# A block-diagonal step for the state chain, and the loads, norm and tanh of a head pair moved beside the former pair's inverse

## The chip, the cores and the metric

The kernel runs on one core of a Trainium2 chip. The time is device microseconds of one execution of the whole program; the median of several runs counts. The core's engines are TensorE (PE, matmuls, with PEld for its weight loads), VectorE (DVE), ScalarE (ACT), GpSimd (POOL) and SyncE (SP, which here only issues DMAs). Each takes its instructions strictly in the order in which they stand in its own queue and waits on semaphores where it needs another engine's result. Matmul results go to PSUM, which the kernel divides into banks.

## The reference

One layer of a recurrent decoder for 1024 prompt rows and 64 sample rows (8 groups of 8 rows). A dense input projection gives the columns of three branches; one of them is a recurrence over heads of 64, with a 64x64 state per head.

```python
h = rms_norm(x) * (1 + sc) + sh
P = h @ w_in                       # 1024 x 4352, split in recurrent, pooling and gate columns
# recurrent branch, per head, r, w = decay, k, v, kk (normalised), a per row t:
def step(S, inp):
    sa = einsum("bhvk,bhk->bhv", S, -kk_t)
    S = S * w_t + sa * (kk_t * a_t) + v_t * k_t
    return S, einsum("bhvk,bhk->bhv", S, r_t)
decay = exp(-exp(-softplus(-(w0 + tanh(xw) @ w2)) - 0.5));  a = sigmoid(a0 + xa @ a2)
kk = kk * rsqrt(sum(kk * kk) + 1e-12)
# pooling branch: running means over 2/4/8/16 rows; gates: sigmoid
merged = g_r * (o_r @ w_br_rwkv) + g_p * (o_p @ w_br_pool)
x = x + gt * (merged @ w_out);  x = x + gt * (relu(h2 @ w_ff1)**2 @ w_ff2)
```

The prompt's 1024 rows are handled in 16 chunks of 64 rows: within a chunk the recurrence is solved by a triangular inverse, and from chunk to chunk only the state S is carried: S_next = diag(end) S + (a 64x64 matrix) S + (a term without S), where `end` is the chunk's decay. The 8 heads are taken as 4 pairs: a pair fills the 128 partitions, head 0 in the lower 64 and head 1 in the upper 64.

## The kernel before

**Two kinds of work.** The first half of the run (to some 770 us) is the dense projection: `products` issues, job by job, matmuls of 128x128 weights with 362 or 364 rows (operand names `hx` and `whi`, `wlo`; tag `mm`). The weights come by SP's queue as `wraw`; ScalarE splits off `whi` (L193) and VectorE or GpSimd `wlo` (L194). A job's results are copied out of PSUM by ScalarE, with a tanh for the gate columns (L564), as plain copies for the pooling columns (L582). The recurrent branch needs some of the projected columns and runs beside the rest of them: `heads` (below), `chains`, and `pools`, in which VectorE forms the sums of the windows (L601, L602) and small products `px,plw` follow. After these, products on the merged rows (`mr`), the output projection and the MLP follow in the second half.

**What sets the order.** TensorE's order is written by hand through a clock of planned TensorE time, `Pace`: the dense stream (`back`) and the three other tasks (`fore`) are generators; a task that yields a number of nanoseconds is taken up again when that much planned matmul time has gone by, one that yields a function when that is true. `Pace.warm(t)` also waits for enough dense work before. The other engines' orders come from a scheduler, which lays the instructions by its own estimates. So the numbers in the yields set the place of a piece of work between the dense matmuls, and the other queues follow.

**The pairs.** For pair f, `front(f)` loads the projected columns k, kk, wa and r from DRAM, shifts and mixes rows through transposes (`spread`, L177 with `kct`, and `wt,sw` products), forms the norm (`rinv`, L347 to L362: products with two columns, a square root on ScalarE, a reciprocal on VectorE, and copies of the result by ScalarE, L360), takes two tanh out of PSUM (L677, L680), and then works out the decay by a scan (L698) and the decayed keys `bk` (L710, L711). `scores` and `unit` make the score products `ra,bk` for chunks of four, read out by VectorE (L794, L795) and ScalarE (L800, L802). `inverse` and `level` solve the triangles, `affine` makes for each of two units of 8 chunks the matrices of the state step: its `first` makes `w` and `uv`, its `second` two groups of products `ab,at` read out by ScalarE (L960) and VectorE (L961). `sample(f)` does the 64 sample rows (products `x,z` and `ab,uv`, readers L1028 to L1067), `post(f)` the normalisation and output gate of the pair (L1113 to L1118).

`heads` puts them together: `lead` (front and scores of f) runs merged with `sample(f-1)`, then `main` (inverse, level, affine of f) merged with `post(f-1)`. `chains` runs `chain(f)` from the time that the first unit of pair f is ready: 16 steps, one each 2300 ns of planned time (1500 in the last pair), so beside `lead` of the next pair. One step, for both heads of a pair (`pn` collects the next state, `py` the output rows, `ra[:, i, 1]` holds the matrix and `ra[:, i, 0]` the output weights):

```python
for hs in HB:                                   # HB: partitions 0-63, 64-127
    self.mm(pn[hs, at], ra[hs, i, 1, :], S[hs, :], ...)
nc.vector.scalar_tensor_tensor(S1, S, end[:, c:c + 1], pn[:, at], op0=ALU.mult, op1=ALU.add)
for hs in HB:
    self.mm(py[hs, at], S[hs, :], ra[hs, i, 0, :], ...)
```

**PSUM.** Tag `mm` has four banks (dense), `wc` two (pn and py of the chain), `w` two, for everything else of the heads: a group of products with tag `w` must wait until the group before the last one has been read out.

## Time and profile before

| what | value |
| --- | --- |
| median of three runs | 1656.83 us (1656.82 to 1659.11) |
| profiled execution | 1654.8 us, of it the span 1653.0 |
| TensorE busy | 1597.1 us, 97% of the span |
| VectorE, ScalarE, GpSimd busy | 1040.3, 721.7, 364.6 us |
| mean granted TensorE clock | 0.991 |

The profile is of one execution. Busy time is the time in which an engine runs an instruction; a line such as "PE w L170 <- ACT wt L677: 5.7, 8, 2.0" among the waits says that TensorE (its matmuls of tag w, issued at line 170) stood idle for 5.7 us in total, 8 times, at most 2.0 us at once, until ScalarE's instruction of line 677, which writes or reads wt, was done. In a timeline row stand the start, the duration, the engine, line and operation, output and inputs, the sizes, and in brackets the idle time before and what ended it. Line numbers are those of the kernel before, unless said otherwise; from L363 on the changed kernel's are 2 higher, from L680 some 10 to 16, from the chain on 21 to 23.

### The profile page before, as it was taken

How to read it: one execution, taken by the hardware profiler on the slowest of the kernel's cores; microseconds unless marked ns; L12 is line 12 of the kernel's file. 1: busy time of each engine (PE TensorE's matmuls, PEld its weight loads, DVE VectorE, ACT ScalarE, POOL GpSimd, SP SyncE). 2: the span in 40 equal slices, each digit the busy share in tenths (PEclk: the TensorE clock that was granted, in tenths of full speed). 3: DMA queues.
4: the chain of work that ended last, by engine and by line, in shares of the span. 5: the costliest groups of instructions: out<-in, count | busy, mean ns of one | idle time of the engine just before them, and what ended most of it. 6: DMA issues, size and time to landing. Idle time of an engine off the chain costs nothing.

```text
span 1653.0 us, 35432 instructions
## 1 busy us (share of the span) xinstructions
PE 1597.1 (97%) x14331; PEld 1488.8 (90%) x14331; DVE 1040.3 (63%) x1800; ACT 721.7 (44%) x1414; POOL 364.6 (22%) x459
## 2 busy tenths in 40 slices
PE   6999999999999999999999999999999999999997
PEld 3989878887888889979989999999999999999997
DVE  5686547744675466334553696777555677877866
ACT  5543333343334333412233475545444765553323
POOL 3320101100000000001631332323233342521231
PEclk9999999999999999999999999999999999999999
DMA  9333413331332242375976455666665965675313
GB/s 338 111 110 135 139 48 119 117 102 67 113 109 92 80 136 102 103 295 174 348 251 227 131 181 180 220 226 240 232 222 204 347 202 190 195 247 182 99 39 109
DMA packets 123333, 279.43 MB, mean 169 GB/s; under 512 B 16769, under 2 KB 31105, under 8 KB 123169
## 3 DMA queue, kind: packets, MB, share of 16 engines
q1 hardware_dynamic: 107808, 228.52, 40.4%
q0 software_dynamic: 9312, 32.41, 5.9%
q10 hardware_dynamic: 6048, 16.23, 2.8%
q8 instruction: 113, 1.85, 0.5%
q14 instruction: 52, 0.42, 0.1%
HBM read 198.15 MB, written 78.95 MB: 168 GB/s over the span
## 4 chain that ended last, share of the span: by engine, by line
PE 82%; DVE 7%; ACT 4%; DMA 3%; issue 3%; POOL 1%; SPq 0%; DVEq 0%; ACTq 0%; POOLq 0%
PE mm L170 36%; PE pr L170 30%; PE w L170 11%; PE wc L170 4%; DMA wraw<-in_w_out 1%; PE w L177 1%; DVE hx L1729 1%; DMA x<-in_xT 1%; ACT whi L193 1%; DVE wlo L194 1%; DVE bk L711 0%; DVE wt L698 0%; POOL wlo L194 0%; DVE bk L710 0%; DMA wr<-in_w_ff 0%
## 5 line engine op out<-in xcount | busy, mean ns | idle before, releaser
L170 PE MATMUL mm<-hx,whi 128*128 128x362 f32 (+1 forms) x1920 | 507.8, 346 | 6.8 <-ACT px L564 2.9
L170 PEld LDWEIGHTS mm<-hx,whi 128*128 128x128 f32 x1920 | 334.0, 190 | 43.2 <-issue 18.5
L170 PE MATMUL pr<-mr,whi 128*128 128x272 f32 x1792 | 336.5, 287 | 0.6 <-DVE hx L1729 0.6
L170 PE MATMUL mm<-hx,wlo 128*128 128x362 f32 (+1 forms) x960 | 316.1, 329 | 0.0
L170 PEld LDWEIGHTS pr<-mr,whi 128*128 128x128 f32 x1792 | 280.7, 188 | 2.8 <-issue 2.8
L170 PE MATMUL pr<-mr,wlo 128*128 128x272 f32 x896 | 257.9, 288 | 0.2 <-DVE wlo L194 0.2
L193 ACT ACTIVATE whi<-wraw 128x512 fp32r<-128x512 f32 x186 | 116.9, 630 | 232.3 <-PE mm L170 68.9
L194 DVE TENSOR_TENSOR wlo<-wraw,whi 128x512 fp32r<-128x512 f32 x145 | 112.1, 773 | 121.1 <-ACT whi L193 120.9
L170 PEld LDWEIGHTS mm<-hx,wlo 128*128 128x128 f32 x960 | 182.9, 190 | 0.0
L170 PE MATMUL pr<-hx,whi 128*128 128x272 f32 x896 | 168.7, 287 | 1.4 <-DVE rs L1924 0.8
L170 PEld LDWEIGHTS pr<-mr,wlo 128*128 128x128 f32 x896 | 168.6, 188 | 0.4 <-DVE wlo L194 0.4
L170 PE MATMUL mm<-mr,whi 128*128 128x272 f32 (+4 forms) x736 | 152.3, 301 | 0.0
L170 PEld LDWEIGHTS pr<-hx,whi 128*128 128x128 f32 x896 | 140.3, 188 | 2.6 <-ACT whi L193 1.0
L193 ACT ACTIVATE whi<-wr 128x512 fp32r<-128x512 f32 x138 | 86.4, 628 | 112.6 <-PE pr L170 80.4
L170 PE MATMUL pr<-hx,wlo 128*128 128x272 f32 x448 | 128.9, 288 | 0.0
L170 PEld LDWEIGHTS mm<-mr,whi 128*128 128x128 f32 x736 | 119.2, 188 | 3.0 <-issue 2.5
L170 PE MATMUL mm<-mr,wlo 128*128 128x272 f32 (+4 forms) x368 | 110.2, 299 | 0.0
L194 POOL TENSOR_TENSOR wlo<-wraw,whi 128x512 fp32r<-128x512 f32 x41 | 55.3, 1349 | 245.8 <-ACT whi L193 245.6
L194 DVE TENSOR_TENSOR wlo<-wr,whi 128x512 fp32r<-128x512 f32 x103 | 77.2, 752 | 17.4 <-ACT whi L193 17.3
L170 PE MATMUL pr<-t,whi 128*128 128x272 f32 x448 | 84.6, 287 | 0.0
L170 PEld LDWEIGHTS pr<-hx,wlo 128*128 128x128 f32 x448 | 84.3, 188 | 0.0
L170 PEld LDWEIGHTS pr<-t,whi 128*128 128x128 f32 x448 | 70.2, 188 | 0.8 <-issue 0.8
(398 smaller groups left out, 2704.9 us busy)
## 6 DMA issues: line engine op xcount, KB each, us to landing
wr<-in_w_ff SPq DMA_DIRECT2D x137, 256.0 KB, 3.4
hid<-d_ch POOLq DMA_DIRECT2D x72, 272.0 KB, 3.7
wraw<-in_w_ff SPq DMA_DIRECT2D x71, 256.0 KB, 3.1
wraw<-in_w_in SPq DMA_DIRECT2D x68, 256.0 KB, 3.0
d_ch<-hx SPq DMA_DIRECT2D x52, 272.0 KB, 3.7
hid<-in_w_ada_mlp SPq DMA_DIRECT2D x24, 512.0 KB, 6.6
d_th<-px SPq DMA_DIRECT2D x22, 544.0 KB, 2.9
wt<-d_x SPq DMA_DIRECT2D x20, 544.0 KB, 4.3
```

Of the source, the lines that this page charges most:

```text
L170: return self.nc.tensor.matmul(out, lhsT, rhs, **kw)
L177: self.nc.tensor.transpose(out, in_, ident)
L193: nc.scalar.activation(hi, raw, AF.Copy)
L194: (nc.gpsimd if pool else nc.vector).tensor_tensor(lo, raw, hi.bitcast(F32), op=ALU.subtract)
L1729: nc.vector.tensor_tensor(acc, acc, v, op=ALU.add)
```

## The change

Four edits, in the order of the code.

1. `rinv` ends with a tanh of one column, whose result nobody reads; it loads ScalarE's table for the tanh.
2. `front` is split. `front(f)` keeps the loads, mixing, norm and tanh, with 1900 and 2000 ns after a tanh instead of 1300; the scan and the decayed keys become `burst(f)`, in which pieces are 1800, 1700 and 1400 ns apart for f > 0 (they had none between). `heads` runs `front(0)` ahead of all, and `front(f+1)` behind `post(f-1)`, so beside inverse, level and affine of pair f; `lead` holds `burst` and `scores`. The first unit of the scores starts 3000 instead of 9000 ns later for f > 0, and `warm` asks 12000 ns instead of 8000.
3. The chain's step has one product per output in place of two: `pn` from the block-diagonal 128x128 matrix `ra[:, i, 1:3]`, to which the chunk's decay has been added on the diagonal, and `py` from `sbd`, a 128x128 tile with the two heads' states on its diagonal. ScalarE copies the new state from PSUM to S, GpSimd copies its two halves into `sbd`.
4. `affine` builds that matrix: `ra` has a third plane, `at` now lies there, GpSimd makes the diagonal of the decay (`dg`) and clears the off-diagonal blocks, VectorE adds the products to the diagonal in place of ScalarE's copy. In `first` the copy of one half of `uv` goes from VectorE to ScalarE.

```diff
@@ -352,3 +352,4 @@
             self.mm(ps[:, 2 * i:2 * i + 2], x[:, b:b + 128], self.kc("hsel"), start=True, stop=True)
-        r = self.cp.tile([P, 9, 2], F32, tag="rh", bufs=3, name=self.nm("rh"))[:, :k, :]
+        r = self.cp.tile([P, 10, 2], F32, tag="rh", bufs=3, name=self.nm("rh"))
+        last, r = r[:, 9, 0:1], r[:, :k, :]
         f = r.rearrange("p k h -> p (k h)")
@@ -361,2 +362,3 @@
             i += m
+        nc.scalar.activation(last, R[-1][:, 0:1], AF.Tanh)
         return [x[:, o:o + 128] for x in R for o in range(0, x.shape[1], 128)]
@@ -664,3 +666,3 @@
         t1, tha = self.wt(), self.wt()
-        yield self.pace.warm(8000 if f else 11000)
+        yield self.pace.warm(12000 if f else 11000)
 
@@ -680,3 +682,3 @@
             nc.scalar.activation(tha[:, c0:c0 + n], ps[:, :n], AF.Tanh, bias=self.hp[:, 4 + f:5 + f], scale=0.5)
-            yield 1300
+            yield 1900 if c0 else 2000
         yield X(f)
@@ -684,2 +686,10 @@
         nc.sync.dma_start(r, self.d_x[f])
+        self.cur = dict(k=k, kk=kk, t1=t1, tha=tha, r=r)
+
+    def burst(self, f):
+
+        nc, io = self.nc, self.io
+        X = lambda b: lambda: ("X", b) in self.done
+        k, kk, t1, tha, r = (self.cur[x] for x in ("k", "kk", "t1", "tha", "r"))
+        step = lambda t: t if f else 0
         e = self.row(self.p1, "e", 1, w=1112)
@@ -691,4 +701,2 @@
         bk = self.p1.tile([P, NC, 2, 64], F32, tag="bk", bufs=1, name=self.nm("bk"))
-        if f:
-            yield lambda: ("c", f - 1, 0) in self.done
         for c0, n in FH:
@@ -698,2 +706,3 @@
             nc.vector.tensor_tensor_scan(t, self.kscan[:, s], t, 0.0, ALU.mult, ALU.add)
+            yield step(1800)
             m = min(n, NPR - c0)
@@ -709,2 +718,3 @@
             for h, hs in enumerate(HB):
+                yield step(1700)
                 nc.vector.tensor_tensor(bk[hs, cs, h, :], cut(x[hs]), cut(t[hs]), op=ALU.mult)
@@ -713,3 +723,5 @@
                 self.cur = dict(bk=bk, end=end, kk=kk, r=r, ev=ev, es=es, z=self.z, qs={})
-                self.ra(self.cur, 0)
+                if f == 0:
+                    self.ra(self.cur, 0)
+            yield step(1400)
         nc.gpsimd.tensor_copy(end[:, 0:16], ev[:, :, 64])
@@ -722,2 +734,5 @@
         self.cur.update(q=q, v=v)
+        if f:
+            yield lambda: ("c", f - 1, 0) in self.done
+            self.ra(self.cur, 0)
 
@@ -728,3 +743,3 @@
         cs = slice(8 * u, 8 * u + C)
-        ra = self.p1.tile([P, C, 2, 64], F32, tag=f"ra{C}", bufs=2 if u < 2 else 1, name=self.nm("ra"))
+        ra = self.p1.tile([P, C, 3 if u < 2 else 2, 64], F32, tag=f"ra{C}", bufs=2 if u < 2 else 1, name=self.nm("ra"))
         d["qs"][u] = dict(ra=ra)
@@ -775,3 +790,3 @@
         if prompt:
-            Q["at"] = tl("at", [64])
+            Q["at"] = ra[:, :, 2, :]
             strict, incl = self.kc("strict"), self.kc("incl")
@@ -779,3 +794,3 @@
             strict, incl = self.kc("strict8"), self.kc("incl8")
-        yield 9000 if u == 0 else 3000 if u == 1 else 2000
+        yield (3000 if f else 9000) if u == 0 else 3000 if u == 1 else 2000
         for a in range(0, C, 4):
@@ -788,3 +803,3 @@
                     self.mm(ps[:, i * 128:(i + 1) * 128], bk[hs, c0 + a + i, :, :].rearrange("p s j -> p (s j)"),
-                            ra[hs, a + i, :, :].rearrange("p s j -> p (s j)"), start=True, stop=True)
+                            ra[hs, a + i, 0:2, :].rearrange("p s j -> p (s j)"), start=True, stop=True)
             for h, (hs, ps) in enumerate(zip(HB, pss)):
@@ -944,3 +959,3 @@
             nc.scalar.activation(w, cut(pw), AF.Copy)
-            nc.vector.tensor_copy(uv[HB[1], :, 0, :], cut(pu[HB[1], :]))
+            nc.scalar.activation(uv[HB[1], :, 0, :], cut(pu[HB[1], :]), AF.Copy)
             nc.scalar.activation(uv[HB[0], :, 1, :], cut(pu[HB[0], :]), AF.Copy)
@@ -956,7 +971,17 @@
                             tile_position=(os.start, hs.start))
-            for a, ps in enumerate(pss):
-                pv = ps.rearrange("p (c s j) -> p c s j", s=2, j=64)
-                us = slice(4 * a, 4 * a + 4)
-                nc.scalar.activation(ra[:, us, 1, :], pv[:, :, 1, :], AF.Copy)
-                nc.vector.tensor_tensor(ra[:, us, 0, :], ra[:, us, 0, :], pv[:, :, 0, :], op=ALU.add)
+            dg = cut(self.hv())
+            for h, hs in enumerate(HB):
+                nc.gpsimd.tensor_tensor(dg[hs], self.kc("ident")[hs, hs].unsqueeze(1).to_broadcast([64, 8, 64]),
+                                        d["end"][hs, 8 * u:8 * u + 8].unsqueeze(2).to_broadcast([64, 8, 64]), op=ALU.mult)
+            for h, hs in enumerate(HB):
+                nc.gpsimd.memset(ra[hs, :, 2 - h, :], 0.0)
+            for k in (1, 0):
+                for a, ps in enumerate(pss):
+                    pv = ps.rearrange("p (c s j) -> p c s j", s=2, j=64)
+                    us = slice(4 * a, 4 * a + 4)
+                    if k:
+                        for h, hs in enumerate(HB):
+                            nc.vector.tensor_tensor(ra[hs, us, 1 + h, :], pv[hs, :, 1, :], dg[hs, us, :], op=ALU.add)
+                    else:
+                        nc.vector.tensor_tensor(ra[:, us, 0, :], ra[:, us, 0, :], pv[:, :, 0, :], op=ALU.add)
 
@@ -972,3 +997,3 @@
         nc = self.nc
-        end = d["end"]
+        both = self.sbd
         S = None
@@ -985,13 +1010,11 @@
             for i in range(8):
-                c = 8 * u + i
                 at = slice(i * 64, (i + 1) * 64)
-                S1 = self.sm.tile([P, 64], F32, tag="S", bufs=3, name=self.nm("S"))
-                if S is None:
-                    nc.vector.tensor_copy(S1, pn[:, at])
-                else:
-                    for hs in HB:
-                        self.mm(pn[hs, at], ra[hs, i, 1, :], S[hs, :], start=False, stop=True, skip_group_check=True)
-                    nc.vector.scalar_tensor_tensor(S1, S, end[:, c:c + 1], pn[:, at], op0=ALU.mult, op1=ALU.add)
-                    for hs in HB:
-                        self.mm(py[hs, at], S[hs, :], ra[hs, i, 0, :], start=False, stop=True, skip_group_check=True)
+                S1 = self.sm.tile([P, 64], F32, tag="S", bufs=2, name=self.nm("S"))
+                if S is not None:
+                    self.mm(pn[:, at], ra[:, i, 1:3, :].rearrange("p s j -> p (s j)"), S, start=False, stop=True, skip_group_check=True)
+                nc.scalar.activation(S1, pn[:, at], AF.Copy)
+                if S is not None:
+                    self.mm(py[:, at], both.rearrange("p s j -> p (s j)"), ra[:, i, 0, :], start=False, stop=True, skip_group_check=True)
+                for h, hs in enumerate(HB):
+                    nc.gpsimd.tensor_copy(both[hs, h, :], S1[hs, :])
                 S = S1
@@ -1144,5 +1167,6 @@
 
+        yield from self.front(0)
         for f in range(4):
             def lead():
-                yield from self.front(f)
+                yield from self.burst(f)
                 yield from self.scores(f, self.cur)
@@ -1156,5 +1180,9 @@
                 self.y3 = self.wt()
-            fill = self.post(f - 1) if f else self.ada_fill()
             self.ds[f] = d
 
+            def fill():
+                yield from self.post(f - 1) if f else self.ada_fill()
+                if f < 3:
+                    yield from self.front(f + 1)
+
             def main():
@@ -1164,3 +1192,3 @@
 
-            yield from self.both(main(), fill)
+            yield from self.both(main(), fill())
         yield from self.sample(3, d)
@@ -1277,2 +1305,4 @@
         nc.gpsimd.memset(self.kscan[:, NPR:NT:8], 0.0)
+        self.sbd = sm.tile([P, 2, 64], F32, name="sbd")
+        nc.gpsimd.memset(self.sbd, 0.0)
         self.tt = sm.tile([P, 2, 16, 16], F32, name="tt")
```

How the queues move. First the state. VectorE's queue before, beside the chain of pair 1 (S_4815 is the state of a step, wc its PSUM, bk, ra and e belong to pair 2's front):

```order
L736 SCALAR_TENSOR_TENSOR ra_5154<-wt_4475,e_4741 64x64
L737 TENSOR_TENSOR ra_5154<-wt_4739,e_4741 64x64
L710 TENSOR_TENSOR bk_4745<-wt_4474,wt_4481 64x9x64
L711 SCALAR_TENSOR_TENSOR bk_4745<-wt_4482,wt_4481 64x9x64
L710 TENSOR_TENSOR bk_4745<-wt_4474,wt_4481 64x9x64
L711 SCALAR_TENSOR_TENSOR bk_4745<-wt_4482,wt_4481 64x9x64
L994 SCALAR_TENSOR_TENSOR S_4815<-S_4788,end_2952,wc_4678 128x64
```

ScalarE's queue after, beside the chain of pair 1 (L679 and L682 are the two tanh, L709 to L712 the exponentials of the decay, all of pair 2):

```order
L679 ACTIVATE wt_4245<-w_4573,hp 128x288
L682 ACTIVATE wt_4246<-w_4576,hp 128x288
L643 ACTIVATE d_4430<-w_4579,part 128x362
L1015 ACTIVATE S_4584<-wc_4312 128x64
L709 ACTIVATE e_4604<-wt_4245 128x8x64
L711 ACTIVATE e_4604<-wt_4245 128x8x8
L712 ACTIVATE wt_4245<-wt_4245 128x576
L1015 ACTIVATE S_4629<-wc_4312 128x64
```

The state's step has left VectorE and stands in ScalarE's queue between the tanh and the exponentials. GpSimd's queue at about that place, with the two copies into `sbd` per step:

```order
L1019 COPY sbd<-S_4390 64x64 [waits PE_49,Activation_49]
L1019 COPY sbd<-S_4390 64x64 [waits Pool_49]
L594 COPY pn_4426<-px_4043 128x15 [waits DMAHW1_49,Activation_49,Pool_49]
L595 COPY pn_4426<-psm_4044 128x120 [waits DMASW6_49,Activation_49]
L579 DMA psm_4950<-in_spool 128x8x15 [waits DMASW0_49,DVE_49]
L977 MEMSET ra_3428 64x8x64 [waits PE_49]
L1019 COPY sbd<-S_4490 64x64 [waits PE_49,Activation_49]
```

Second, TensorE where the second unit of pair 1's `affine` meets its chain. Before:

```order
L170 MATMUL w_4426<-px_3956,plw_3712 128x362
L170 MATMUL w_4430<-ab_3447,at_3450 64x128 x8
L170 MATMUL w_4431<-ab_3447,at_3450 64x128 x8
L170 MATMUL wc_4337<-S_4414,ra_2965 64x64 x2
L170 MATMUL wc_4338<-ra_2965,S_4414 64x64 x2
L170 MATMUL w_4458<-px_3956,plw_3712 128x298
```

After:

```order
L170 MATMUL w_4455<-ab_3431,ra_3428 64x128 x8
L170 MATMUL w_4456<-ab_3431,ra_3428 64x128 x8
L177 MATMUL w_4484<-kct,wt_4239 128x128 x4
L170 MATMUL wc_4312<-S_4390,ra_2984 128x64
L170 MATMUL wc_4313<-ra_2984,sbd 128x64
L170 MATMUL mm_4448<-hx_346,whi_4249 128x362
```

Behind the two groups of `affine` now stands a group of transposes of pair 2's front (L177), which takes the bank of w_4455. VectorE's queue there, after (L603, L604 are the pooling sums; L984, L986 read w_4455):

```order
L603 TENSOR_TENSOR d_4430<-px_4043 128x1038
L604 TENSOR_TENSOR psm_4432<-psm_4044 128x183
L603 TENSOR_TENSOR px_4431<-d_4430 128x1036
L604 TENSOR_TENSOR psm_4435<-psm_4432 128x181
L984 TENSOR_TENSOR ra_3428<-w_4455,hv_4473 64x4x64 x2
L986 TENSOR_TENSOR ra_3428<-ra_3428,w_4455 128x4x64
```

The readers of w_4455 stand behind the pooling sums, and are three instructions where they were one of VectorE and one of ScalarE. Third, TensorE at the sample's first products `x,z` of pair 1. Before:

```order
L170 MATMUL w_4646<-wt_4479,sw_4472 128x512
L170 MATMUL w_4649<-wt_4479,sw_4472 128x512
L170 MATMUL mm_4596<-hx_350,whi_4490 128x362
L170 MATMUL mm_4596<-hx_351,whi_4490 128x362
L170 MATMUL mm_4596<-hx_350,wlo_4491 128x362
L170 MATMUL w_4661<-x_4485,z 64x64 x2
```

After:

```order
L170 MATMUL w_4847<-ra_4807,bk_4608 128x128
L170 MATMUL w_4846<-ra_4807,bk_4608 128x128
L170 MATMUL w_4847<-ra_4807,bk_4608 128x128
L170 MATMUL w_4866<-x_4613,z 64x64 x2
L170 MATMUL wc_4698<-S_4828,ra_3428 128x64
L170 MATMUL wc_4699<-ra_3428,sbd 128x64
```

Before, `x,z` took the bank of the products `wt,sw` whose reader is a tanh; now it takes that of the score products of pair 2.

## The prediction

> **What bounds the kernel.** I read the page first: the span and the busy shares.
>
> ```profile
> span 1653.0 us, 35432 instructions
> PE 1597.1 (97%) x14331; PEld 1488.8 (90%) x14331; DVE 1040.3 (63%) x1800; ACT 721.7 (44%) x1414; POOL 364.6 (22%) x459
> ```
>
> TensorE is busy 97% of the span, so a change can win only in its idle time, in time at a lower clock, or in its own work. Next I asked by stages: 50 to 750 us holds the four head pairs, and the short windows are those there with a low granted clock.
>
> ```profile
> core 0: us, PE busy (x) PEld busy (x) DVE busy (x) ACT busy (x) POOL busy (x), PEclk, DMA share, GB/s
> 50.00:750.00 700.00, 674.70 (x7395) 595.97 (x7394) 405.14 (x771) 269.05 (x586) 61.32 (x121) 0.99 0.35 117
> 235.00:240.00 5.00, 5.00 (x33) 4.43 (x33) 1.36 (x3) 0.81 (x3) 0.00 (x0) 0.78 0.08 28
> 400.00:405.00 5.00, 4.45 (x24) 3.91 (x25) 2.32 (x5) 1.75 (x5) 0.00 (x0) 0.66 0.50 164
> 425.00:430.00 5.00, 5.00 (x36) 4.63 (x36) 2.32 (x4) 1.83 (x4) 0.00 (x0) 0.67 0.56 167
> 560.00:570.00 10.00, 10.00 (x56) 9.37 (x57) 2.23 (x6) 2.83 (x7) 0.00 (x0) 0.66 0.05 15
> ```
>
> Idle are 700 - 674.7 = 25.3 us. The four clock windows, all in stretches where a chain and the next pair's front share TensorE, lose 5 x 0.22 + 5 x 0.34 + 5 x 0.33 + 10 x 0.34 = 7.8 us. That is the whole purse, some 33 us or 2%. Then the waits of TensorE, over the whole run:
>
> ```profile
> PE w L170 <- ACT wt L677: 5.7, 8, 2.0
> PE wc L170 <- DVE S L994: 4.3, 4, 2.8
> PE mm L170 <- ACT px L564: 2.9, 3, 1.8
> ```
>
> Nothing is to be had from the heads ending earlier:
>
> ```profile
> L177 PE MATMUL w<-kct,sw x4: 272/272/329, 359.4 to 771.3; 128*128 128x128 f32 x4
> ...
> L170 PE MATMUL mm<-mr,whi x736: 277/287/427, 831.4 to 1636.0; 128*128 128x272 f32 x128, 128*128 128x364 f32 x32, 128*128 128x448 f32 x8, 128*128 128x384 f32 x8
> ```
>
> The last transpose of the heads' work is at 771 us and the first product on the merged rows at 831; between them is projection work that TensorE does anyway.
>
> **The change, part by part.**
>
> *A. Matmuls of the chain.* A step was four 64-wide products (two array corners at once) and becomes two 128-wide ones. The first fence is an isolated step, the second nine products with 128x128 weights and two columns.
>
> ```profile
> 220.76 0.32 PE L170 MATMUL mm<-hx,wlo 128*128 128x362 f32 x1
> 221.01 0.33 PE L170 MATMUL wc<-S,ra 64*64 64x64 f32 x4
> 221.17 0.28 PE L170 MATMUL wc<-ra,S 64*64 64x64 f32 x4
> 221.39 0.43 PE L170 MATMUL mm<-hx,whi 128*128 128x362 f32 x1
> ```
>
> ```profile
> 75.69 0.32 PE L170 MATMUL mm<-hx,wlo 128*128 128x362 f32 x1
> 75.86 2.06 PE L170 MATMUL w<-kct,wt 128*128 128x2 f32 x18
> 77.78 0.59 PE L170 MATMUL mm<-hx,whi 128*128 128x364 f32 x2
> ```
>
> Dense products start 0.17 us apart (75.69 to 75.86), so the old step took 221.39 - 220.76 - 0.17 = 0.46 us, of which 221.01 - 220.93 = 0.08 us is the change of tile size. A pass with 128x128 weights costs (77.78 - 75.86) / 18 = 0.107 us; the new step has four: 0.43 us. Against 0.46 that gains 0.03; a step beside other narrow work paid no size change before (0.38) and loses 0.05. Over 60 steps: between -1.8 and +3.0. I take 0, since both kinds are common in the order.
>
> *B. The state leaves VectorE.* The largest wait in the chain, row by row:
>
> ```profile
> 423.84 0.75 DVE L711 SCALAR_TENSOR_TENSOR bk<-wt,wt 64x576 f32<-64x576 f32 x1
> 424.63 0.28 DVE L994 SCALAR_TENSOR_TENSOR S<-S,end,wc 128x64 f32<-128x64 f32 x1
> ...
> 424.96 0.48 PE L170 MATMUL wc<-S,ra 64*64 64x64 f32 x4 [2.80 <-DVE S L994]
> ```
>
> The 0.28 us step stood behind the next pair's decayed keys (L711 is the last of them) and TensorE waited 2.80 us. On ScalarE, which is at 44%, no such run stands ahead: -4.3 us, the row's total. The clock window 425 to 430 follows that wait directly; with it go its 5 x 0.33: -1.7.
>
> *C. The tables and the banks.* First the gate's wait, which has a table load at its end:
>
> ```profile
> 398.73 1.28 ACT L564 ACT_TABLE_LOAD   x1
> 400.02 0.47 ACT L564 ACTIVATE px<-mm 128x362 f32<-128x362 f32 x1
> ```
>
> TensorE waited 1.8 us (the longest of the L564 row) for a copy out of PSUM that stood behind a table load. After the change the norm ends with the load and that gate's copy is elsewhere: -1.8. The four added loads of 1.28 us fall on an engine that is 44% busy: 0, and 5.1 if nothing covers them.
>
> Then the waits whose tile is `w`. This tag has two banks; a group of products must wait until the group before the last has been read out.
>
> ```profile
> 242.65 1.28 ACT L677 ACT_TABLE_LOAD   x1
> ...
> 244.78 0.33 PE L170 MATMUL w<-x,z 64*64 64x64 f32 x4 [2.05 <-ACT wt L677]
> ```
>
> The sample's products x,z read nothing that L677 makes: they waited 2.05 us for the bank that the tanh (and its table load) still read. All such waits but the smallest:
>
> ```profile
> PE w L170 <- DVE wt L1115: 1.9, 2, 1.0
> ...
> PE w L170 <- DVE px L642: 1.2, 3, 0.6
> ...
> PE w L177 <- ACT z L928: 0.7, 1, 0.7
> PE w L177 <- ACT wt L360: 0.7, 1, 0.7
> PE w L170 <- ACT at L944: 0.7, 1, 0.7
> ```
>
> With L677's 5.7 they make 10.9 us. I counted in the two orders the places where under 1.7 us of TensorE's work (by the durations of the timeline) lies between a group and the next but one: 26 before, 36 after. At the old mean of 10.9 / 26 = 0.42 us the new order has 15.1 us. By place it is more, since the new ones stand behind slow readers. (a) The sample's x,z and ab,uv stand, in pairs 2 and 3, right behind the score products ra,bk. How late such a bank comes free:
>
> ```profile
> 307.89 1.16 PE L170 MATMUL w<-ra,bk 64*128 64x128 f32 x14 [0.28 <-ACT iv L800]
> ...
> 308.98 0.42 DVE L794 TENSOR_TENSOR ab<-w,kct 128x256 f32<-128x256 f32 x1
> ...
> 309.82 0.27 ACT L800 ACTIVATE iv<-w 32x128 f32<-32x128 f32 x1 [1.98 <-DVE ak L795]
> ...
> 310.26 0.60 ACT L800 ACTIVATE iv<-w 32x128 f32<-32x128 f32 x2
> ```
>
> The products end at 309.05, the first bank is read out at about 310.5: 1.5 us. With 0.1 us of other work between that costs two x,z 1.5 each, with three dense products two ab,uv 1.0 each, and gates and scores of pair 2 another 2.1: 7.1. (b) The front's transposes for the shift stand right behind the affine part's second products in three pairs, whose readers are now two adds and a third on VectorE.
>
> ```profile
> L961 DVE TENSOR_TENSOR ra<-ra,w 128x256 f32<-128x256 f32 x16 | 6.6, 420 | 15.0 <-ACT ra L960 14.7
> ```
>
> Three of 0.42 are 1.26, and some 0.3 until TensorE sees it; 0.9 lies between: 0.7 at three places, 2.1. In pair 1 VectorE's order has the pooling sums ahead of those adds:
>
> ```profile
> L601 DVE TENSOR_TENSOR d<-px 128x1038 f32<-128x1038 f32 x4 | 4.9, 1232 | 0.0
> ```
>
> From the end of the norm products: ScalarE has its root, a weight copy and the pooling copies done at 1.6 us; the sums (two of 1.23, two of 0.4) end at 4.8, the adds at 6.1; TensorE is there at 1.5 + 1.7 = 3.2. So 2.9 there, and 1.2 for the second bank behind the next 1.23 us sum: 4.1. (c) Ten smaller places of 0.3 to 0.9: 5.4. Together 18.7; from before stay the first front's 0.9 and L1115's 1.9: 21.5. I take the middle of 15.1 and 21.5, 18.3, which is +7.4 against 10.9. Bounds: all new places quiet, 10.9 less L677's later 4.8, so -4.8; and +10.6.
>
> *D. The new path of the state.* TensorE, then ScalarE's copy, then two copies on GpSimd into the block-diagonal weights, then the next step's second product. Prices:
>
> ```profile
> L533 ACT ACTIVATE px<-mm 128x64 f32<-128x64 f32 x13 | 3.0, 228 | 0.0
> ```
>
> ```profile
> L540 POOL COPY ns<-px x14: 192/1276/5337, 63.9 to 290.9; 128x8 f32<-128x8 f32 x14
> ```
>
> The three durations are least, median and longest in ns: a GpSimd copy is 0.19 us alone, 1.28 in the median (mostly beside VectorE's pooling work), 5.3 at worst. Alone, the path is about 0.4 (product to the start of the copy) + 0.23 + 2 x 0.25 + 0.1 = 1.2 us. The least work between two steps of pairs 0 to 2 is fifteen dense products, 15 x 0.166 = 2.5 us, plus 0.6 us of chain products: 1.9 us to spare. Pair 3 has 9 to 12 products: 0.9 to 1.4 us to spare. So two median waits (2 x 1.1 us more) are about the point where TensorE begins to wait. [...]
>
> [...]
>
> *E. The rest.* The diagonal is built on GpSimd (two multiplies of 1.3 us a unit at most, the longest of its small copies above) while at least 4.9 us of TensorE's work stands ahead of the first step that needs it: 0, and if that cover is short 1 us a unit, 8 in all. GpSimd's DMA issue for the pooling state (0.9 us) now stands between two copies of the state and waits for the sums of (b), as TensorE does there: nothing on top. SP's queue has the same transfers; the front's loads now stand ahead of weight loads, which have some 36 dense products (6 us) of buffered work: 0, at worst 2 us each in three pairs.
>
> **Sum.** -4.3 - 1.7 - 1.8 + 0 + 7.4 + 4.2 = +3.8 us. The profiled execution took 1654.8 us (span 1653.0 and 1.8 around it) and goes to 1658.6; it is 2.0 us under the median, 1656.83, so the median goes to 1660.6, say 1661.
>
> **Rivals.**
>
> 1. *The banks come free in time (faster).* The places are counted with TensorE never late and the readers in their worst order; VectorE and ScalarE are at 63 and 44%. If the new places are quiet and the copies on time, -4.3 - 1.7 - 1.8 - 4.8 = -12.6: 1644, and with half the new waits 1650. It decides from a total of bank waits and late copies below 18.7 us (10.9 and the 7.8 gained). For it: dense products lie around nearly every step, and the sample is freed of the tanh. Against: the order has ten more tight places.
> 2. *GpSimd's copies come late (slower still).* [...] If the pair of copies is on average 0.3 us beyond its spare time in 45 steps of pairs 0 to 2, TensorE loses 13.5 us, 9.3 more than in the sum: 1670; at 0.4, 1675. It decides from about 2.2 us for the two copies on average.
> 3. *No net change.* The new banks cost the old mean (+4.2 for 7.4) and the copies half of what I took: 1655 to 1659.
>
> Clock windows move any of these: a dip like those above is 1.7 us, and two more or fewer make 3.4. [...]
>
> **Numbers.** A difference of 0.2% (3.3 us) is about what a measurement can tell from none. The forecast (1658 to 1666) has 0.30, of it 0.06 within 0.2%; rival 1 0.34; rival 2 0.20; rival 3 0.16, of it 0.10 within, 0.03 on each side. That makes faster 0.37, same 0.16, slower 0.47. I give 1661 and, reaching into rivals 1 and 2, 1646 to 1673; the forecast's own range is 1658 to 1666.
>
> **What would show it.** In the profile after: no wait of the chain's first product for VectorE; waits of its second product for GpSimd's copy, few and under 1 us; waits of `w` products, x,z and ab,uv for ScalarE's L815, the transposes of L177 for VectorE's L986, of 1 to 3 us each; no TensorE wait that ends with a table load before the gate's copy; chain steps of 0.43 us. The forecast is wrong if the waits whose tile is `w` sum to less than 12 us, or if GpSimd's copies stand among the largest releasers of TensorE.

## The result: slower by 1.1%

The changed kernel takes 1676.4 us (median of five runs, 1671.96 to 1677.23) where the kernel before takes 1656.82 us (1654.95 to 1659.11): ratio 1.0107, 95% interval 1.0089 to 1.0125 (this ratio and those below differ by about 0.1% from the quotients of the medians). Two far longer executions, one of the kernel before (3100.07 us) and one of the version with a hold of 1000 ns below (3946.29 us), count in no ratio here. The direction was as forecast; the size was not: 19.6 us for the forecast 4, and outside the range (1646 to 1673). The profiled execution took 1671.96 us, with a span of 1670.2 for 1653.0, 17.2 us more. From the page of the changed kernel, the span and the busy times:

```profile
span 1670.2 us, 35269 instructions
PE 1599.3 (96%) x14091; PEld 1503.0 (90%) x14091; DVE 1036.4 (62%) x1760; ACT 737.8 (44%) x1483; POOL 430.0 (26%) x620
```

TensorE works 2.2 us longer and has 15 us more of idle time. Where the time is lost is told by the two starts of the products on the merged rows, which end the first half (831.4 us before; the row of the changed kernel):

```profile
L170 PE MATMUL mm<-mr,whi x736: 278/287/428, 843.0 to 1652.9; 128*128 128x272 f32 x128, 128*128 128x364 f32 x32, 128*128 128x448 f32 x8, 128*128 128x384 f32 x8
```

They begin at 843.0 us for 831.4: 11.6 us are lost up to there, and 17.2 - 11.6 = 5.6 us behind it, in code that no edit touches. The waits of TensorE in the changed kernel (us in total, times, longest; L815 and L817 read out the score products, L644 the pooling's products, L1138 those of `post`, L986 and L959 those of `affine`, L610 and L614 are the pooling sums):

```profile
...
PE w L170 <- ACT iv L815: 7.5, 5, 1.7
PE w L170 <- DVE px L644: 4.9, 3, 2.5
PE pr L170 <- DVE hx L1759: 3.6, 3, 1.7
PE w L170 <- DVE wt L1138: 3.2, 4, 1.0
...
PE mm L170 <- ACT px L566: 1.8, 3, 1.2
PE wc L170 <- POOL sbd L1019: 1.7, 2, 1.1
...
PE w L170 <- ACT z L922: 1.6, 1, 1.6
PE w L170 <- DVE px L614: 1.5, 1, 1.5
PE w L177 <- DVE ra L986: 1.4, 2, 0.7
PE w L177 <- DVE zf L610: 1.3, 1, 1.3
PE w L170 <- ACT ra L959: 1.2, 2, 0.7
...
PE wc L170 <- ACT S L1015: 0.9, 1, 0.9
```

VectorE's state step (4.3 us before) is gone from the list, GpSimd's copies cost 1.7 us, and most of the rest bears the tile `w`. Summed from the timeline, from 50 us to the first product on the merged rows, and beside it the time that windows of 5 us lose by a granted clock under 1 (these two figures, called w waits and clock loss, are given for every kernel below; a wait without a releaser's name counts too if its product is a `w`). Each is of one profiled execution, which need not be a typical one: that of the changed kernel is the fastest of its five, 4.4 us under their median.

```
                        w waits   waits of mm   of wc   clock loss   first product on merged rows
before                    13.9        6.8        4.3       10.2         831.4
changed                   28.9        3.1        2.7       10.2         843.0
```

So 15.0 us of new `w` waits, less 5.3 us saved in the other two columns: 9.7 of the 11.6 us. The clock loses the same.

One of the new places in the timeline of the changed kernel, the sample's x,z right behind the score products of pair 2:

```profile
415.99 1.16 PE L170 MATMUL w<-ra,bk 64*128 64x128 f32 x16
417.19 0.42 DVE L809 TENSOR_TENSOR ab<-w,kct 128x256 f32<-128x256 f32 x1 [3.31 <-PE w L170]
417.53 0.41 DVE L810 TENSOR_TENSOR ak<-w,kct 64x256 f32<-64x256 f32 x1
417.86 0.40 DVE L809 TENSOR_TENSOR ab<-w,kct 128x256 f32<-128x256 f32 x1
418.03 0.27 ACT L815 ACTIVATE iv<-w 32x128 f32<-32x128 f32 x1 [3.90 <-DVE ak L810]
...
418.47 0.59 ACT L815 ACTIVATE iv<-w 32x128 f32<-32x128 f32 x2
418.79 0.33 PE L170 MATMUL w<-x,z 64*64 64x64 f32 x4 [1.64 <-ACT iv L815]
```

The products end at 417.15; two readers on VectorE and then three on ScalarE (L815, L817, L815; the rows of the two banks are mixed) follow one after the other, and 1.64 us later the bank is free. TensorE had nothing else in its order.

### The profile page after: what moved, and what is told of

It reads as the page before. It is cut to its first block, busy times and chain, and to the rows that moved or that the text cites. A ratio compares the mean times of both kernels' runs of the same rounds, so it can differ in the third digit from the quotient of the medians.

```text
span 1670.2 us, 35269 instructions
## 1 busy us (share of the span) xinstructions
PE 1599.3 (96%) x14091; PEld 1503.0 (90%) x14091; DVE 1036.4 (62%) x1760; ACT 737.8 (44%) x1483; POOL 430.0 (26%) x620
## 4 chain that ended last, share of the span: by engine, by line
PE 54%; DVE 3%; DMA 3%; ACT 3%; issue 3%; POOL 1%; SPq 0%; ACTq 0%; DVEq 0%; POOLq 0%
PE pr L170 30%; PE mm L170 18%; PE w L170 4%; PE wc L170 2%; DMA wraw<-in_w_out 1%; DVE hx L1759 1%; DMA hx<-d_opl 1%; ACT whi L193 0%; DVE wlo L194 0%; POOL wlo L194 0%; DMA hid<-d_u 0%; DMA d_ch<-hid 0%; ACT hx L1682 0%; DVE hx L1928 0%; PE w L177 0%
## 5 line engine op out<-in xcount | busy, mean ns | idle before, releaser
L170 PEld LDWEIGHTS mm<-hx,whi 128*128 128x128 f32 x1920 | 335.6, 191 | 34.9 <-issue 18.3
L1019 POOL COPY sbd<-S 64x64 f32<-64x64 f32 x128 | 47.3, 369 | 161.0 <-ACT S L1015 148.6
L194 DVE TENSOR_TENSOR wlo<-wr,whi 128x512 fp32r<-128x512 f32 x103 | 76.7, 747 | 16.4 <-ACT whi L193 16.3
```

What stands on the lines that cost most here:

```text
L170: return self.nc.tensor.matmul(out, lhsT, rhs, **kw)
L194: (nc.gpsimd if pool else nc.vector).tensor_tensor(lo, raw, hi.bitcast(F32), op=ALU.subtract)
L1019: nc.gpsimd.tensor_copy(both[hs, h, :], S1[hs, :])
```

## The experiments

**Each part alone.** The hunks of the diff fall into two groups that do not need one another.

```diff
 e1_front_only: before, with
+ the hunks of rinv (tanh), front, burst, warm, the yields, heads
 e2_chain_only: before, with
+ the hunks of ra's third plane, first, second, chain, sbd
```

> Only the moved front (front beside the former pair's inverse, burst, the yields, the tanh at the end of the norm); chain and affine as in the kernel before. Theory (the loss is waits for the two w banks, made by the new places of the front, the scores and the sample): the waits whose tile is w sum to 22 to 30 us, as in the changed kernel (28), against 12 before, and the time is 8 to 18 us above before. Rival (the new path of the state and its matmuls cost the time): w waits near 12, time within 4 us of before.

Measured: 1673.56 us, ratio 1.0089 (1.0072 to 1.0105), 16.4 us over the kernel before, as the theory had it; w waits 30.6, just over its 22 to 30; clock loss 13.6.

> Only the block-diagonal chain and its affine part; the front stays where it was. Theory: the chain's matmuls cost 3 to 4 us (0.44 us a step for 0.38, read in the changed kernel), the wait for the state on VectorE (4.3) goes, GpSimd's copies cost 2: time within 5 us of before, w waits 10 to 16 us. Rival (the new path costs the time): 10 to 18 us above before, waits for sbd of more than 5 us.

Measured: 1659.78 us, ratio 1.0022 (1.0003 to 1.0041); w waits 14.2, and for GpSimd's copies:

```profile
PE wc L170 <- POOL sbd L1004: 2.7, 3, 1.4
```

The moved front alone makes the whole of the new `w` waits and 0.9% of the 1.07%; the new chain costs 0.2%. Its clock loss was 18.8 us, 8.6 more than before, which is more than the 2.6 us between the medians; why the clock dips more often there is open. In the profiled executions the chain alone takes 7.7 us more (1660.7 for 1653.0), of which only 1.4 lie in the first half (832.8 for 831.4): its second half takes 827.9 us for 821.6, to which the experiment "The same kernel again" comes back. The rival that blamed GpSimd is out.

**The distance between groups.** If the loss is banks that are asked for too soon, a hold that keeps the order of each task and only lets dense products and steps of the chain in between must bring it back. It holds the heads and the pooling, not the chain. `ends` holds the planned time at which the last groups with tag `w` ended (the main lines of the edit, with a comment added):

```diff
 class Pace:
+    def close(self):
+        self.ends += [self.t] * self.open       # open: groups with tag w since the last close
+        self.open = 0
+    def free(self, i):
+        return i not in self.hold or self.t - self.ends[-2] >= 1700
...
-                if r() if callable(r) else r <= self.t:
+                if self.free(i) and (r() if callable(r) else r <= self.t):
                     try:
                         r = next(fore[i])
+                        self.close()
...
 def both(self, a, fill):
             ready = now()
+            pace.close()
-            if not ready:
+            if not ready or not pace.free(1):
```

> The changed kernel, but a piece of the heads or the pooling is taken up only when 1700 ns of planned TensorE time have gone by since the last group but one with tag w; places with under 1.7 us between fall from 36 to 22, those under 1.0 us from 25 to 7. Theory: w waits fall from 28 to 8 to 14 us, the time by 12 to 20 us to 1656 to 1664. Rival (the banks are only where another lateness shows): waits move to other names, the time stays within 5 us of the changed kernel.

Measured: 1644.87 us, ratio to the kernel before 0.9915 (0.9898 to 0.9931). This version beats both kernels, and by more than expected: it is 11 us under the range of 1656 to 1664. Its page and the longest of its waits (line 179 is 170 of the others, 186 is 177; L933 and L372 are copies of `level` and of the norm):

```profile
span 1640.0 us, 35260 instructions
PE 1594.5 (97%) x14091; PEld 1498.4 (91%) x14091; DVE 1031.6 (63%) x1760; ACT 738.4 (45%) x1483; POOL 426.8 (26%) x620
```

```profile
...
PE mm L179 <- issue: 3.3, 1, 3.3
PE w L186 <- ACT wt L372: 3.1, 2, 2.4
PE w L179 <- ACT z L933: 2.4, 2, 1.4
...
PE w L179 <- DVE px L655: 1.5, 2, 1.0
...
PE w L179 <- ACT iv L826: 0.2, 1, 0.2
```

w waits 10.1 (28.9 without the hold); the waits for the score products' readers fall from 7.5 to 0.2 us, and no wait for a state or for `sbd` is left. The first half ends at 818.3 us, 24.7 earlier: 18.8 from `w` waits, 0.8 from the other two columns (5.0 us for 5.8), 3.4 from the clock (6.8 for 10.2). The second half takes 821.7 us for 827.2, another 5.5, which the theory had not counted. The work is the same: 14091 products.

> The kernel before with the same hold; places under 1.7 us fall from 26 to 15. Theory: w waits fall from 12 to 4 to 8 us, the time by 4 to 8 us to 1649 to 1653. Rival: no change beyond 2 us, since the waits of before had other causes.

Measured: 1654.66 us, ratio 0.9978 (0.9963 to 0.9992); w waits 8.3. The expected 4 to 8 us came as 2.5, and the waits show what took the rest:

```profile
PE wc L179 <- DVE S L1005: 12.1, 6, 3.7
```

With the hold the old chain waits nearly three times as long for its state on VectorE (4.3 before). What the banks give back (5.6 us), the state takes (7.8 us); the profiled execution, 1656.58 us, is one of the slower of its twelve.

> The moved front alone (the old chain) with the hold of 1700 ns. Theory: the bank waits go (30 to 8 to 12 us), but the chain's state step stays in VectorE's queue, and its waits rise to some 8 to 14 us as in the spaced kernel before (12): time 1650 to 1658. Rival (the hold's gain does not need the new chain): 1640 to 1648, as the spaced changed kernel.

Measured: 1649.05 us, ratio 0.9944 (0.9928 to 0.996); w waits 11.4. The state's waits were 3.9 us, not 8 to 14, and the time lies between the two ranges, 1 us under the theory's and 1 us over the rival's: the long waits for the state come where the front stands beside the chain and the hold is on, not with the hold alone.

> The block-diagonal chain alone (the front where it was) with the hold. Theory: w waits fall from 14 to 6 to 9 us, no waits for the state on VectorE: time 1648 to 1654, some 6 to 10 us under the chain alone. Rival (the front must be moved for the hold to pay): 1655 to 1660.

Measured: 1656.28 us, ratio 0.9998 (0.9979 to 1.0016); w waits 10.1, clock loss 17.1. The rival holds: the w waits fall by 4 us, not quite to the expected 6 to 9, and the time is above 1654, 3.5 us under the chain alone. The clock loss is again some 7 us over that of the kernel before, and the waits for GpSimd's copies, 4.3 us, are the largest of all versions.

The eight versions as ratios to the kernel before (each against the runs of it that are on record beside it):

```
                      without the hold              with the hold of 1700 ns
before                1                             0.9978 (0.9963 to 0.9992)
chain alone           1.0022 (1.0003 to 1.0041)     0.9998 (0.9979 to 1.0016)
front alone           1.0089 (1.0072 to 1.0105)     0.9944 (0.9928 to 0.9960)
both                  1.0107 (1.0089 to 1.0125)     0.9915 (0.9898 to 0.9931)
```

The moved front costs 0.9% where its groups fall too close and gains 0.3% over the held kernel before where they don't. The chain costs 0.2% in three of the four pairs, two of them with intervals that overlap, and gains 0.3% on top of the moved front with the hold, where the two intervals just touch. Nothing of the work differs between the columns.

**Other lengths of the hold.** The number 1700 in `free` becomes 1000 or 1400.

> The changed kernel with a hold of 1000 ns. Theory: the places nearer than 1.0 us go (25 to 4), those of 1.0 to 1.7 us stay, and banks behind score products come free 1.5 us late: w waits 11 to 17 us, time 1646 to 1655. Rival (only the order's shift, not the distance, gives the gain): the same as with 1700, 1643 to 1646, or as without.

Measured: 1648.02 us (the median of five, 1642.45 to 1649.11), ratio 0.9935 (0.9912 to 0.9958). The time is in the theory's range; there is no profile of these executions, so its 11 to 17 us of w waits are not tested.

> The changed kernel with a hold of 1400 ns. Theory: w waits 9 to 14 us, time 1643 to 1650, between 1000 and 1700. Rival: no order by the hold's length.

Measured: 1649.7 us, ratio 0.9952 (0.9935 to 0.9969), w waits 11.2. Both lie over the 1644.87 of 1700 ns, but not in the order of their lengths: the interval of 1400 ns is just clear of that of 1700, and 1000 ns can be told from neither. Of the 10.6 us between the profiles with 1400 and 1700, 7.1 lie in the second half (828.8 us for 821.7). So an order by length beyond 1000 ns is not shown; most of the gain is there at 1000, which takes away the places under 1 us (25 to 4).

**Two places alone.** Only the sample's two groups behind the score products are held.

```diff
         yield 9500 if f < 3 else 8000
+        yield lambda: self.pace.t - self.pace.ends[-2] >= 1700
         px = self.ps("w")
...
         yield 4500 if f < 3 else 2500
+        yield lambda: self.pace.t - self.pace.ends[-2] >= 1700
         py = self.ps("w")
```

> The changed kernel with only the sample's x,z and ab,uv products held until 1700 ns of planned TensorE time lie behind the last group but one; all else keeps its place. Theory: the four waits of 1.64, 1.66, 1.63 and 0.94 us behind the score products (5.9 in all) go, up to 2 us come back at the score products behind them: time 3 to 6 us under the changed kernel. Rival (the readers are late anyway): the same waits under the name of the next w group, no change.

Measured: 1672.94 us, ratio 1.0085 (1.0064 to 1.0106), 3.5 us under the changed kernel's median, at the low end of what was expected and within the noise of the two. The waits for the score products' readers fell by 5.7 us as foretold (7.5 to 1.8), but others rose: the w waits sum to 29.5 us, no less than the 28.9 of before the edit, and the clock loss was 18.8. So the four waits went and as much came back elsewhere, much of it in one place:

```profile
PE w L179 <- ACT ra L970: 7.6, 2, 6.9
...
PE w L179 <- ACT iv L826: 1.8, 1, 1.8
```

The wait of 6.9 us in the timeline of this kernel, with ScalarE's rows there (L673 squares k for the norm of pair 3's front, L970 reads out a `w` bank):

```profile
538.81 1.39 ACT L673 ACTIVATE wt<-wt,part 128x512 f32<-128x512 f32 x2 [6.51 <-DMA wt<-d_x]
540.10 0.57 ACT L970 ACTIVATE ra<-w 128x512 f32<-128x512 f32 x1
```

```profile
540.73 1.36 PE L179 MATMUL w<-px,plw 128*128 128x298 f32 x2 [6.93 <-ACT ra L970]
```

ScalarE stood 6.5 us for the front's own load, with the bank's reader behind it. In the changed kernel the same place costs 2.5 us: L662 (the same square) waits for the load, L643 (the pooling's copy out of PSUM) stands behind it, L644 on VectorE behind that, and `ab,ra` wants the bank.

```profile
534.99 1.39 ACT L662 ACTIVATE wt<-wt,part 128x512 f32<-128x512 f32 x2 [2.79 <-DMA wt<-d_x]
536.28 0.54 ACT L643 ACTIVATE d<-w,part 128x362 fp32r<-128x362 f32 x1
```

```profile
537.50 1.27 PE L170 MATMUL w<-ab,ra 64*64 64x128 f32 x16 [2.47 <-DVE px L644]
```

The load is issued only at 529.36, behind the stores of `post`:

```profile
528.98 0.33 SPq L1162 DMA_DIRECT2D d_orh<-wt  x1
529.36 0.42 SPq L660 DMA_DIRECT2D wt<-d_x  x1
```

To take that wait away, the square was set 7000 ns behind the load:

```diff
         nc.sync.dma_start(k, self.d_x[4 + f])
+        yield 7000 if f else 0
```

> The kernel with the held sample, and 7000 ns of planned TensorE time between the front's load of k and ScalarE's square of it (for pairs 1 to 3; the whole front shifts behind it). Theory: the 6.9 us wait of px,plw at 541 us stood behind ScalarE's wait for that load; it goes, ScalarE's waits for wt<-d_x fall from 13.2 to under 4 us, and the time falls by 4 to 9 us against the held sample alone. Rival (the wait was for the bank's own products or for the pooling's weights): a wait of 4 to 7 us stays at px,plw, time within 3 us.

Measured: 1664.16 us, ratio 1.0041 (1.0015 to 1.0067). By the ratios that is 0.44%, some 7 us, under the held sample alone (the two ran on different chips, and their intervals just overlap), but not by what was expected: ScalarE's waits for `wt<-d_x` were still 9.8 us in all (13.2 before the edit). The wait at 541 is gone, and the w waits fell from 29.5 to 19.6, but the whole front moved too. Nor does the profile show where the gain comes from: it is of the slowest of the ten executions (1673.04 us), no faster than that of the held sample alone (1673.74), and what its w waits gave up went to the clock (22.2 us lost for 18.8) and to a longer second half (829.6 us for 825.1). A wait of 5.9 us stands at another px,plw. The profile names no releaser for it; by the rows it is none for a bank: the pooling's sums (L624, L625) stood on VectorE behind the inverse's transposes (L899, L901), and the product starts when L625 is done, at 513.22.

```profile
509.15 1.07 DVE L899 STREAM_TRANSPOSE hv<-iv 128x512 f32<-128x512 f32 x1 [0.37 <-ACT wt L1142]
510.11 1.00 DVE L901 STREAM_TRANSPOSE iv<-iv 128x512 f32<-128x512 f32 x1
510.96 1.20 DVE L624 SCALAR_TENSOR_TENSOR px<-px,px 128x1024 f32<-128x1024 f32 x1
...
512.95 0.16 DVE L625 COPY px<-zf 128x15 f32<-128x15 f32 x1
```

So not every `w` wait is a bank. Single places can be removed, but in these two runs the shift made a new order with its own late readers; what worked was to keep the distance everywhere.

**The tanh at the end of the norm.**

```diff
-        nc.scalar.activation(last, R[-1][:, 0:1], AF.Tanh)
```

> The changed kernel without the tanh at the end of the norm, whose result nobody reads; table loads fall from 22 to 16. Theory: the load comes back ahead of the front's first tanh and of gate copies, each 1.28 us later: waits for L678 and the gate's copies rise by 2 to 5 us, time 0 to 5 us over the changed kernel. Rival (the added loads only lengthen ScalarE's queue, which reads out the banks): time 2 to 5 us less.

Measured: 1681.53 us, ratio 1.0145 (1.0125 to 1.0165), 5.1 us over the changed kernel's median, at the upper end of the theory's range; the two intervals touch. The waits for the front's tanh rise from 1.0 to 2.6 us (the wait for L678), those for the gate's copies do not (0.8 for 1.8), and the clock loss goes from 10.2 to 17.1. So the six added table loads (1.28 us each in the profile of the changed kernel) cost nothing and seem to pay, but most of what they pay stands in the clock, and that it is owed to them is not shown.

**The same kernel again.**

> The changed kernel once more, unedited, for a second profile. Theory: w waits 27 to 31 us and the first product on the merged rows at 841 to 850 us again; the second half (from that product to the end), 827.2 us in the first profile for 821.6 before, moves by several us from execution to execution. Rival (the second half is slower by the change): it takes 826 to 830 us again.

Measured: 1674.97 us, ratio 1.0107 (1.0077 to 1.0136). The first half repeats to 0.3 us in w waits (29.2) and begins the merged rows at 841.8. The second half took 829.8 us, as the rival has it: 5.6 and 8.2 us over the kernel before in the two profiles, though nothing in it is edited. Some 3 us are these waits; the first row is of the kernel before, whose L1729 is L1759 here, the second of this run:

```profile
PE pr L170 <- DVE hx L1729: 0.6, 2, 0.3
```

```profile
PE pr L170 <- DVE hx L1759: 3.2, 3, 1.6
```

Clock dips in its first 120 us take 1.7 us in the first profile (0.66 over 5 us) and 3.3 in the second; before there are none. The other profiles say with which part it goes. In the four versions with the old chain the second half takes 820.5 to 824.4 us, and the dips there 0 to 1.7. In the nine with the new chain it takes 824.9 to 829.8 and the dips 1.7 to 6.5, but for the one with the hold of 1700 ns (821.7 and 1.7). The waits for L1759 explain it only in part: the version with the hold of 1400 ns has them too (3.4 us), the chain alone (827.9 us) does not. So the longer second half goes with the new chain in eight profiles of nine, not with the moved front (822.6 alone). There is only one profile of the kernel before, and what brings the difference about is open.

## Why the prediction was right and wrong

Measured against the terms of the sum, in the profiled executions (17.2 us where the sum had 3.8), two things make the difference of 13.4: the banks, with 7.6 us more than their term, and the second half, with 5.6 us where the sum has no term. The others cancel to about nothing. Most of the signs came as foretold (waits for L815 and L986, none of the chain's first product for VectorE), so for the first half the mechanism was right and its size was not.

- **The banks: right in kind, too small.** The step that failed is the term "+7.4" of part C: it measured +15.0, 28.9 us of w waits against 13.9. By place the prediction had 21.5 us, by count 15.1, and took the middle, 18.3, against 10.9. The 10.9 left out the rows under 0.7 us and the two that name no reader (1.3 and 0.8). The rows that were priced by hand were good in sum, 15.8 us for 16.1: x,z 1.64 and 1.63 us (foretold 1.5 each), ab,uv 1.66 and 0.94 (1.0 each), the three places behind `affine` that wait for L986 0.68 each (0.7 each; the 0.3 us in it "until TensorE sees it" were the author's estimate, while in the trace of before a product starts 0.05 to 0.15 us after the end of what it waited for), `post` 1.9 as before, the first front 0.5 for 0.9. Pair 2's gates and scores took more, 1.64 and 1.85 (2.1 in all), pair 1's two places less, 1.29 and 0.73 for 4.1. All that is missing by place lies in the "ten smaller places", 13.1 us for 5.4. Four waits make 7.1 of it, the 2.47 at 537.50 shown above and these:

```profile
310.80 0.85 PE L170 MATMUL w<-px,plw 128*128 128x364 f32 x2 [1.58 <-issue]
...
458.07 0.85 PE L170 MATMUL w<-px,plw 128*128 128x364 f32 x2 [1.46 <-DVE px L614]
...
515.10 1.92 PE L170 MATMUL w<-hv,ao 32*32 32x32 f32 x64 [1.55 <-ACT z L922]
```

  By the rows the two px,plw waited for no bank: the pooling sums that they read were late on VectorE (L614 ends at 310.70 and 457.81, shortly before each starts). So the places were priced with every reader and every operand on time, and the middle with the old average, which came from places with quick readers, took off 3.2 us more.
- **The front's loads: missed.** Part E had them at 0, "at worst 2 us each". They are issued behind the stores of `post`, and ScalarE stands for them with a bank's reader behind it: 2.5 us at 537 us in the changed kernel, 6.9 in the kernel with the held sample. The prediction looked at what the loads delay on SP's queue, not at who stands in line behind the instruction that waits for them.
- **The copies on GpSimd: too dear.** 4.2 us were taken, the last term of the sum, which no run shows; measured were 1.7, two waits of 1.07 and 0.68 us in 60 steps. Least, median and longest of the 128 copies in ns:

```profile
L1019 POOL COPY sbd<-S x128: 228/234/1262, 215.5 to 749.8; 64x64 f32<-64x64 f32 x128
```

  The median of 1.28 us from which the price came was of copies that ran beside a pooling sum on VectorE (in the kernel before the copy at 113.30 starts 0.07 us after L543's sum of 1.29 us); here it is 0.23. Rival 2 named about the right time (1670 to 1675) with the wrong cause, which is luck.
- **The state off VectorE: right.** The 4.3 us went; 0.9 us came back as one wait for ScalarE's copy. The 1.7 us of clock that were to go with it did not: 10.2 us are lost in both profiles, before in the windows of 5 us at 400, 425 (the one behind the 2.80 us wait), 515, 560 and 565 us above all (0.65 to 0.71), after at 370, 470 and 735 (0.66) and 515 (0.50). That such a dip is owed to a wait just ahead of it was the author's assumption and is not shown: in the window ahead of 560 us before, and of 370 after, TensorE is busy throughout (5.00 of 5 us).
- **The chain's products: right.** An isolated step in the timeline of the changed kernel:

```profile
413.31 0.33 PE L170 MATMUL mm<-hx,wlo 128*128 128x362 f32 x1
413.48 0.33 PE L170 MATMUL wc<-S,ra 128*128 128x64 f32 x2
413.64 0.39 PE L170 MATMUL wc<-ra,sbd 128*128 128x64 f32 x2
413.84 0.58 PE L170 MATMUL mm<-hx,whi 128*128 128x362 f32 x2
```

  413.84 - 413.48 = 0.36 us for the forecast 0.43 and the 0.46 of before. Behind narrow products it is 0.47. From start to start, waits left out, all steps together take nearly 4 us more and the dense products some 4 us less: about nothing, as the sum had it. Where a dense product stands alone in its row ahead of a step, it took 0.26 us from start to start before, ahead of 64x64 products, and takes 0.17 in the changed kernel, ahead of 128x128 ones (medians of 37 and 32 places). That this change of tile size makes up the 4 us is likely, not shown.
- **The gate's wait: right in part.** The wait of 1.84 us is gone, but another of 1.19 stands at 685.31, and ScalarE still had a table load for a gate's copy in its queue, at 681.55. The row of the gate's copies falls from 2.9 to 1.8 us, 1.1 for the 1.8 of the sum. The waits with tile `mm` fell by 3.7 us in all; the rest are waits for other copies and were not counted.
- **The second half: not in the sum.** The prediction looked at the span up to the merged rows and put what follows at nothing, without a reason. It measured 5.6 us, 3.6 in waits of tile `pr` and 1.7 in clock dips; what brings them about is open.
- What is left, some 2 us, lies in the time that the first half's own products take from start to start, most of it in the products `ab,ra` (those of pair 1, 32 in one row, take 2.70 us for the 1.96 of other pairs), perhaps as pieces of waits hidden inside merged rows. It was not split further.

The first rival, banks free in time, is false for the changed kernel, and its time (1644 to 1650) is what the kernel takes when that is made true by the hold: 1644.87.

## What to carry to other kernels

Where an order is written by hand around a small set of buffers, count for each place how much work lies between a group and the next one that takes its buffer, and price it with the readers that this group has, in their queue, not with an average over other places. Moving a piece of work changes these distances everywhere; a rule in the planner that keeps the distance (here one comparison against the end of the last group but one) decided whether the move paid: with it the change gains 0.85%, without it it loses 1.1%. On the kernel before, the rule alone gained 0.2%. And compare the whole run: a third of what was lost here lay in a half that no edit touched. For a load that is moved, ask which engine stands for it and what else that engine is to read out.

## What the runs showed of the hardware that was not expected

Two copies of 64x64 on GpSimd, one behind the other, took 0.52 us in the median of 64 pairs and 1.05 at the upper quartile, beside a VectorE that is busy 57% of that time (397.21 of 700 us). The longest pair, with VectorE's rows there, in the timeline of the changed kernel:

```profile
230.82 0.68 DVE L721 SCALAR_TENSOR_TENSOR bk<-wt,wt 64x512 f32<-64x512 f32 x1
230.92 2.00 POOL L1019 COPY sbd<-S 64x64 f32<-64x64 f32 x2 [0.62 <-PE wc L170]
231.53 1.29 DVE L547 SCALAR_TENSOR_TENSOR d<-d,part,px 128x1024 f32<-128x1024 f32 x1
```

It ends at 232.92, 0.10 us behind L547 (232.82). In the kernel before, nine of the 14 copies of L540 took 1.26 to 1.28 us, and each of them starts 0.06 to 0.08 us after a pooling sum of VectorE (L543 or L545, 1.27 to 1.29 us) and ends 0.05 to 0.07 us behind it. Why a copy takes as long as the sum beside it is not shown. TensorE waited for these copies only twice in 60 steps.
